# Nine octets of loads ahead, seven output buffers and whole-octet masked copies in a linear ReLU attention kernel

## The chip, the cores and the metric

The kernel runs on one core of a Trainium2 chip. Such a core has a matrix engine (TensorE, PE in the profile; its weight loads are PEld), a vector engine (VectorE, DVE), an activation engine (ScalarE, ACT), GpSimd (POOL), a synchronising engine (SyncE, SP) that here issues transfers and waits, and 16 DMA engines that move data between device memory (HBM) and the on-chip memory SBUF. PSUM is the small memory that TensorE writes its results to. The metric is the time of one execution on the device in microseconds (us), as the median of several runs; one more execution is recorded by the hardware profiler.

## The reference

```python
batch, heads, seq, dim = 8, 12, 512, 64        # float32
Q_feat = np.maximum(0, Q)
K_feat = np.maximum(0, K)
KV = np.einsum('bhkd,bhkv->bhdv', K_feat, V)
K_sum = np.sum(K_feat, axis=2)
numerator = np.einsum('bhqd,bhdv->bhqv', Q_feat, KV)
denominator = np.einsum('bhqd,bhd->bhq', Q_feat, K_sum)
return (numerator / (denominator[:, :, :, None] + 1e-10)).astype(np.float32)
```

There are 96 heads of 512 rows of 64 numbers. Each input and the output take 12.58 MB in HBM, so 50.3 MB have to be moved whatever the kernel does.

## The kernel before

**Tiling.** Eight heads make an "octet"; there are 12 octets (`NO`). One octet of an input is one contiguous piece of 1 MB in HBM, loaded by one DMA into a tile of 128 partitions x 2048 elements. The DMAs of GpSimd's queue turn float32 into bfloat16 on the way, so that a load writes 512 KB. In such a tile 16 partitions hold one head, and each partition holds 32 rows (`RQ`) of 64 numbers. Octet 0's K and V alone come over SP's queue as float32, into the output buffers 0 and 1 that nothing else uses yet. An output octet is float32, 1 MB, and is stored by one DMA (the last one by two halves).

**The work on one octet**, step by step:

- `copy_q` (line 198, VectorE) copies Q into the tile `q2`; TensorE transposes it in 16 steps (line 372) and ScalarE's `relu_q` (line 201) writes the result as `qt`.
- `prep_k` (line 183, VectorE) makes masked copies of relu(K) in `kf`; `prep_v` (line 194 on VectorE, line 192 on ScalarE) makes masked copies of V in `vo`. The masks keep the heads that share a partition group apart. There are two masks each (`s`, `t`), and before the change two halves of an octet (`g`), with a tile for each half: four K copies and four V copies of 128 x 1024 elements per octet. One of the V copies runs on ScalarE, seven copies run on VectorE.
- TensorE multiplies them to KV in 64 products (line 381), 32 for each half; ScalarE's `evac_kv` (line 209) brings KV to SBUF.
- TensorE forms the denominators and the eight heads' numerators (both through the helper on line 366, which writes to `ps_kv` and `ps_x`); ScalarE's `copy_ot` (line 217) copies the numerators to `ot`. TensorE transposes them back (line 390) in the next round of its loop.
- `denominators` (lines 222 to 229, VectorE) makes the reciprocals, and `norm` (line 234, VectorE) multiplies them into the output buffer, half an octet at a time. `store` (lines 244 and 247) sends the buffer off.

**What sets the order.** The programs of VectorE, ScalarE, GpSimd and SP are straight lists, written out by `body`, `setup` and `step(i)`; the class `Order` adds semaphore waits from what each operation reads and writes. TensorE runs a loop over the octets (`products`) and waits on counters that the others raise: `q2`, `dn`, `a0`, `d0`, `d1` ahead of the transposes of Q and the two halves of KV, `t0`, `t1` ahead of the transposes back, `n0`, `n1` ahead of the numerators. In `step(i)` octet i is multiplied, octet i-1 is normalised and stored, and octet i+1 is prepared: `first()` (Q copy and four of VectorE's copies) stands ahead of the norm of octet i-1, `second()` (three more) behind the denominators of octet i. In the step of i = 10 (`late`) both parts and ScalarE's V copy stand at the end.

**Queues and buffers.** GpSimd's queue first holds the Q of octet 0, then K, V and Q of octets 1 to 8 (`AHEAD` = 8), then by turns a store and the loads of one octet (store 0, octet 9, store 1, octet 10, store 2, octet 11). Ten semaphores (`LANES`) take turns on that queue, so that a DMA is issued only when the tenth before it has landed. The other stores are issued by SP, and each waits for the V of the last octet to have landed (line 246), then for its own data; SP's DMAs have four semaphores of their own (`sp`), and the last five stores one each (`last`). Octet o is written to output buffer (o + 2) mod `NOUT`, with `NOUT` = 8. At the end of `body` GpSimd waits for all the semaphores `pool` and `sp`; behind the closing handshake of the engines SP waits for the five `last` ones (line 419).

Of the kernel before, what the change touches and what calls it, by code (L numbers as in the profile page):

```python
# [89 lines left out]
def kernel(  # L90
# [16 lines left out]
    U = RQ // 2  # L107
    NO = NH // 8
    assert NO * 8 == NH and R == 16 and RQ == 32
    AHEAD = 8  # L110
    NI = AHEAD
    NOUT = 8
    LANES = 10

    fp32 = mybir.dt.float32
# [13 lines left out]
    ident32 = sb.tile([P, P], fp32, name="ident32")  # L129
    mask = sb.tile([P, 2, 2], fp32, name="mask")  # L130
    mask_h = sb.tile([P, 8, 2], fp32, name="mask_h")
    kf = [sb.tile([P, R, 2, D], bf16, name=f"kf{g}") for g in range(2)]
    vo = [sb.tile([P, R, 2, D4], bf16, name=f"vo{g}") for g in range(2)]
    kvf = sb.tile([P, 8 * 2 * D1], bf16, name="kvd")
    kvd = kvf.rearrange("p (h d) -> p h d", h=8)
    q2 = sb.tile([P, U, P], bf16, name="q2")
# [3 lines left out]
    den = sb.tile([P, RQ], fp32, name="den")  # L140
    rec = sb.tile([P, RQ], fp32, name="rec")
    q_sb = [sb.tile([P, U, P], bf16, name=f"q_sb{i}") for i in range(NI)]
    k_sb = [sb.tile([P, 2, R * D], bf16, name=f"k_sb{i}") for i in range(NI)]
    v_sb = [sb.tile([P, 2, R * D], bf16, name=f"v_sb{i}") for i in range(NI)]
    o_sb = [sb.tile([P, RQ, D], fp32, name=f"o_sb{i}") for i in range(NOUT)]
    ps_kv = psum.tile([P, 2, 512], fp32, name="ps_kv")
    ps_den = ps_kv[:, 1, 256:512]
# [12 lines left out]

    do = Order(nc, sems)

    def kv_src(g):
        o, j = g // 2, g % 2
        kv = (o_sb[0], o_sb[1]) if o == 0 else [x[o % NI].rearrange("p j (r d) -> p (j r) d", d=D) for x in (k_sb, v_sb)]
        key = [("o", c, j) if o == 0 else (c, o % NI, j) for c in ((0, 1) if o == 0 else "kv")]
        return kv[0][:, R * j:R * j + R], key[0], kv[1][:, R * j:R * j + R], key[1]

    def load_q(o):
        do.op("pool", lambda e: e.dma_start(out=q_sb[o % NI].rearrange("p u f -> p (u f)"), in_=Qr[o],  # L170
# [3 lines left out]
    def load(o):  # L174
        i = o % NI
        for n, X, t in (("K", Kr, k_sb), ("V", Vr, v_sb)):
            do.op("pool", lambda e: e.dma_start(out=t[i].rearrange("p j f -> p (j f)"), in_=X[o], single_packet=True),  # L177
                  writes=[(n.lower(), i, 0), (n.lower(), i, 1)], dma=lane("pool"))
        load_q(o)

    def prep_k(g, s):
        src, key, _, _ = kv_src(g)
        do.op("dve", lambda e: e.tensor_scalar(kf[g % 2][:, :, s, :], src, scalar1=0.0,  # L183
                                               scalar2=mask[:, 0, s:s + 1], op0=Alu.max, op1=Alu.mult),
              reads=[key, "mask"], writes=[("kf", g % 2, s)])

    def prep_v(g, t, who, sem=None):
        _, _, src, key = kv_src(g)
        to = vo[g % 2][:, :, t, 2:D + 2]
        m = mask[:, 1, t:t + 1]  # L190
        if who == "act":
            make = lambda e: e.activation(to, src, Act.Copy, scale=m)  # L192
        else:
            make = lambda e: e.tensor_scalar(to, src, scalar1=m, scalar2=None, op0=Alu.mult)  # L194
        do.op(who, make, reads=[key, "mask"], writes=[("vo", g % 2, t)], sem=sem)

    def copy_q(o):
        do.op("dve", lambda e: e.tensor_copy(q2, q_sb[o % NI]), reads=[("q", o % NI)], writes=["q2"], sem="q2")  # L198
# [32 lines left out]
    def norm(o, j):  # L231
        i = (o + 2) % NOUT
        rs = slice(16 * j, 16 * j + 16)
        do.op("dve", lambda e: e.tensor_tensor(o_sb[i][:, rs], ps_x[j].rearrange("p (r d) -> p r d", d=D),  # L234
                                               rec[:, rs].unsqueeze(2).to_broadcast([P, 16, D]), op=Alu.mult),
              reads=[("x", j), "rec"], writes=[("o", i, j)], sem=f"n{j}")

    def store(o, j=None):
        i = (o + 2) % NOUT
        rs = slice(0, RQ) if j is None else slice(16 * j, 16 * j + 16)  # L240
        to, src = Or[o].rearrange("p (r d) -> p r d", d=D)[:, rs], o_sb[i][:, rs]
        keys = [("o", i, h) for h in range(2) if j in (None, h)]
        if o + AHEAD + 1 < NO:
            do.op("pool", lambda e: e.dma_start(out=to, in_=src, single_packet=True), reads=keys, dma=lane("pool"))
        else:
            keys.append(("v", (NO - 1) % NI, 0))
            do.op("sp", lambda e: e.dma_start(out=to, in_=src), reads=keys, dma=lane("sp" if o < NO - 4 else "last"))

    KF = [[("kf", g, 0), ("kf", g, 1), ("vo", g, 0), ("vo", g, 1), ("vo1", g)] for g in range(2)]
    PK = [("pk", 0), ("pk", 1)]  # L250
    QT = [("qt", 0), ("qt", 1)]
    OT = [("ot", 0), ("ot", 1)]
# [4 lines left out]
    def body():  # L257
        for c, X in enumerate((Kr, Vr)):
            do.op("sp", lambda e: e.dma_start(out=o_sb[c].rearrange("p r d -> p (r d)"), in_=X[0]),
                  writes=[("o", c, 0), ("o", c, 1)], dma=lane("sp"))  # L260
        load_q(0)
        memset("pool", ident, 0.0, "ident")
        do.op("pool", lambda e: e.affine_select(out=ident, in_=ident, compare_op=Alu.not_equal, fill=1.0, base=0,
                                                pattern=[[-1, P]], channel_multiplier=1),
              reads=["ident"], writes=["ident"])
        for o in range(1, AHEAD + 1):
            load(o)
            if o == 1:
                setup()
        for o in range(NO + 1):  # L270
            step(o)
        nc.gpsimd.drain()
        for n in lanes["pool"] + lanes["sp"]:
            nc.gpsimd.wait_ge(sems[n], do.count[n])

    def setup():
        for h in range(4):
            for t in range(2):
                do.op("dve", lambda e: e.memset(mask[32 * h:32 * h + 32, 1, t:t + 1], 1.0 if h % 2 == t else 0.0),
                      writes=[("m", h, t), "mask"])  # L280
        for g in range(2):
            ones = vo[g][:, :, :, 1:D4 - 1]
            memset("dve", ones[:, :, :, 0:D + 2:D1], 0.0, ("vo1", g))
            for h in range(4):
                memset("dve", ones[32 * h:32 * h + 32, :, h % 2, 0:D + 2:D1], 1.0, ("vo1", g))
        do.op("dve", lambda e: e.tensor_copy(ident32, ident), reads=["ident"], writes=["ident32"],
              sem="dn")
        for c in range(2):
            do.op("dve", lambda e: e.tensor_reduce(
                out=mask_h[:, :, c], in_=ident32.rearrange("p (h b) -> p h b", h=8), op=Alu.add,  # L290
                axis=mybir.AxisListType.X), reads=["ident32"], writes=[("mh", c), "mask_h"])
        do.op("dve", lambda e: e.tensor_reduce(
            out=mask[:, 0, :], in_=mask_h[:, :, 0].rearrange("p (a s) -> p s a", s=2), op=Alu.add,
            axis=mybir.AxisListType.X), reads=["mask_h"], writes=["mask"])
        prep_k(0, 0)
        prep_k(0, 1)
        prep_v(0, 0, "dve", "d0")
        prep_v(0, 1, "act", "a0")
        do.op("dve", lambda e: e.memset(kvf.bitcast(fp32)[:, 0:4 * D1], 0.0), writes=KVD, sem="n0")
        do.op("dve", lambda e: e.memset(kvf.bitcast(fp32)[:, 4 * D1:], 0.0), writes=KVD, sem="n1")  # L300
        copy_q(0)
        prep_k(1, 0)
        prep_k(1, 1)
        prep_v(1, 0, "dve")
        prep_v(1, 1, "dve", "d1")
        for j in range(2):
            nc.scalar.sem_inc(sems[f"t{j}"], 1)
            do.note("act", "act", (), (), f"t{j}", 1)

    def step(i):  # L310
        r = i + 1
        more, last, late = i + 1 < NO, i == NO, i == NO - 2

        def first():
            copy_q(i + 1)
            prep_k(2 * i + 2, 0)
            prep_k(2 * i + 2, 1)
            prep_v(2 * i + 2, 0, "dve", "d0")
            prep_k(2 * i + 3, 0)

        def second():
            prep_k(2 * i + 3, 1)
            prep_v(2 * i + 3, 0, "dve")
            prep_v(2 * i + 3, 1, "dve", "d1")

        if not last:
            do.looped([("q2", r)], ["q2", "ident"], [("pq", 0)])
# [3 lines left out]
            do.looped([("dn", r), ("a0", r), ("d0", r)], KF[0], PK + ["pd"])  # L331
            do.looped([("d1", r)], KF[1], PK + ["pd"])
            evac_kv()
            if more and not late:
                prep_v(2 * i + 2, 1, "act", "a0")
                first()
        if i > 0:
            o = i - 1
            do.looped([("t0", r), ("t1", r)], [*OT, "ident32"], [("x", 0)])
# [9 lines left out]
        if not last:  # L349
            do.looped([("qt", r), ("ev", r)], [*QT, *KVD], ["pd"])  # L350
            denominators()
            for j in range(2):
                do.looped([(f"n{j}", r)], [*QT, *KVD], [("x", j)])
            copy_ot(0, "act")
            copy_ot(1, "act" if more else "dve")
            if late:
                prep_v(2 * i + 2, 1, "act", "a0")
                first()
            if more:
                second()  # L360

    def products():
        pe = nc.tensor
# [4 lines left out]
        with pe.Fori(0, NO + 2, 1) as r, pe.If(r > 0):  # L368
            with pe.If(r < NO + 1):
# [5 lines left out]
                for g in range(2):  # L375
                    for s in ("dn", "a0", "d0") if g == 0 else ("d1",):
                        pe.wait_ge(sems[s], r)
                    for k in range(R):
                        for h in range(2):
                            ps = slice(64 * h, 64 * h + 64)  # L380
                            x = pe.matmul(  # L381
                                ps_kv[:, h, 0:2 * (D + 2)].rearrange("p (t d) -> p t d", t=2),
                                kf[g][ps, k, :, :].rearrange("p s d -> p (s d)"), vo[g][ps, k, :, 1:D4 - 1],
                                start=(g + k == 0), stop=(g == 1 and k == R - 1), skip_group_check=True)
                    x.then_inc(sems["pe"], 1)
            with pe.If(r > 1):
# [62 lines left out]
```

## Time and profile before

| | |
|---|---|
| runs | 126.50, 126.62 and 127.31 us (median 126.62) |
| the profiled execution | 126.42 us, of which the span from the first to the last instruction is 124.6 us |
| mean granted TensorE clock | 0.934 |
| busy, share of the span | PE 70%, PEld 60%, VectorE 70%, ScalarE 63%, GpSimd 17% |
| DMA queues | software (GpSimd's): 20.97 MB written; hardware (SP's): 11.54 MB written |
| norm of half an octet (line 234, VectorE) | 24 times, 1.214 us |
| masked K copy, bfloat16, 128 x 1024 (line 183, VectorE) | 44 times, 0.458 us |
| masked V copy, bfloat16, 128 x 1024 (line 194, VectorE; line 192, ScalarE) | 33 times, 0.481 us; 11 times, 1.153 us |
| Q copy, bfloat16, 128 x 2048 (line 198, VectorE) | 12 times, 0.683 us |
| a load of GpSimd's queue, from issue to landing | median 24.3 us |
| a store of SP's queue, from issue to landing | median 8.6 us for 1 MB, 3.2 us for half |

The profile shows one execution: for each engine the instructions with their start and length, for each idle time what ended it, and for the 16 DMA engines the share of time in which they moved something. Times within it are counted from the span's start. Durations of instructions on one engine can overlap the next one by some 0.1 us, so that the distance between two starts is often less than the duration.

### The profile page before, as it was taken

How to read it: one execution, taken by the hardware profiler on the slowest of the kernel's cores; microseconds unless marked ns; L12 is line 12 of the kernel's file. 1: busy time of each engine (PE TensorE's matmuls, PEld its weight loads, DVE VectorE, ACT ScalarE, POOL GpSimd, SP SyncE). 2: the span in 40 equal slices, each digit the busy share in tenths (PEclk: the TensorE clock that was granted, in tenths of full speed). 3: DMA queues.
4: the chain of work that ended last, by engine and by line, in shares of the span. 5: the costliest groups of instructions: out<-in, count | busy, mean ns of one | idle time of the engine just before them, and what ended most of it. 6: DMA issues, size and time to landing. Idle time of an engine off the chain costs nothing.

```text
span 124.6 us, 3458 instructions
## 1 busy us (share of the span) xinstructions
PE 87.3 (70%) x1440; PEld 74.8 (60%) x1440; DVE 87.2 (70%) x181; ACT 78.3 (63%) x108; POOL 21.1 (17%) x43
## 2 busy tenths in 40 slices
PE   0000394997997979989797998928966994892900
PEld 0000393996795959779596885915963982781900
DVE  2440947749799898989989799099189359658330
ACT  0000765968988889898888988835773848743000
POOL 5931211321131122113211321000000000000000
PEclk9999999679999999999999999995996799999595
DMA  2999999999999999999999999999999999999971
GB/s 53 400 316 233 212 213 213 213 212 216 216 212 213 213 214 210 213 217 214 212 213 216 368 218 218 334 256 216 301 292 214 268 417 423 426 426 434 426 296 75
DMA packets 7061, 32.56 MB, mean 261 GB/s; under 512 B 784, under 2 KB 784, under 8 KB 5392
## 3 DMA queue, kind: packets, MB, share of 16 engines
q0 software_dynamic: 5328, 20.97, 77.4%
q1 hardware_dynamic: 1728, 11.54, 22.4%
q14 instruction: 4, 0.03, 0.1%
q8 instruction: 1, 0.02, 0.0%
HBM read 37.75 MB, written 12.58 MB: 404 GB/s over the span
## 4 chain that ended last, share of the span: by engine, by line
DMA 58%; DVE 16%; PE 14%; POOL 4%; issue 4%; DVEq 0%; POOLq 0%; SPq 0%
DMA q_sb<-in_Q_dram 20%; DMA v_sb<-in_V_dram 20%; DMA k_sb<-in_K_dram 19%; DVE o_sb L234 8%; PE ps_x L390 5%; PE ps_kv L381 4%; DVE kf L183 3%; PE ps_qt L372 3%; PE ps_x L366 2%; DVE vo L194 2%; POOL q_sb L170 1%; POOL v_sb L177 1%; DVE ot_sb L217 1%; POOL k_sb L177 1%; DVE den L226 1%
## 5 line engine op out<-in xcount | busy, mean ns | idle before, releaser
L234 DVE TENSOR_TENSOR o_sb<-ps_x,rec 128x1024 f32<-128x1024 f32 x24 | 28.3, 1214 | 8.4 <-PE ps_x L390 8.4
L217 ACT COPY ot_sb<-ps_x 128x1024 f32<-128x1024 f32 x23 | 23.2, 1012 | 12.3 <-PE ps_x L366 11.2
L381 PE MATMUL ps_kv<-vo,kf 64*128 64x132 bf16 x768 | 27.1, 229 | 0.6 <-DVE vo L194 0.6
L372 PE MATMUL ps_qt<-ident,q 128*128 128x128 bf16 x192 | 15.9, 248 | 16.5 <-DVE q L198 15.6
L390 PE MATMUL ps_x<-ident,ot_sb 128*128 128x128 f32 x192 | 25.2, 288 | 1.7 <-DVE ot_sb L217 1.7
L381 PEld LDWEIGHTS ps_kv<-vo,kf 64*128 64x128 bf16 x768 | 24.8, 100 | 2.3 <-issue 0.9
L372 PEld LDWEIGHTS ps_qt<-ident,q 128*128 128x128 bf16 x192 | 13.9, 113 | 19.1 <-DVE q L198 15.9
L390 PEld LDWEIGHTS ps_x<-ident,ot_sb 128*128 128x128 f32 x192 | 22.3, 148 | 3.2 <-issue 2.0
L209 ACT CAST kvd<-ps_kv 64x260 bf16<-64x260 f32 x48 | 17.9, 374 | 9.3 <-PE ps_kv L381 8.4
L201 ACT ACTIVATE qt<-ps_qt 128x1024 bf16<-128x1024 bf16 x24 | 23.3, 1030 | 0.6 <-PE ps_qt L372 0.6
L366 PE MATMUL ps_x<-qt,kvd 128*128 128x256 bf16 x96 | 16.0, 296 | 10.9 <-DVE o_sb L234 9.9
L183 DVE TENSOR_SCALAR kf<-k_sb,mask 128x1024 bf16<-128x1024 bf16 x44 | 19.1, 458 | 0.0
L198 DVE COPY q<-q_sb 128x2048 bf16<-128x2048 bf16 x12 | 8.2, 683 | 13.9 <-DMA q_sb<-in_Q_dram 13.9
L366 PEld LDWEIGHTS ps_x<-qt,kvd 128*128 128x128 bf16 x96 | 7.9, 102 | 16.3 <-DVE o_sb L234 15.4
L194 DVE TENSOR_SCALAR vo<-v_sb,mask 128x1024 bf16<-128x1024 bf16 x33 | 14.9, 481 | 0.0
L192 ACT ACTIVATE vo<-v_sb,mask 128x1024 bf16<-128x1024 bf16 x11 | 12.7, 1153 | 0.3
L170 POOL DMA_DIRECT2D q_sb<-in_Q_dram x12 | 6.7, 558 | 16.1 <-DMA v_sb<-in_V_dram 9.5
L177 POOL DMA_DIRECT2D k_sb<-in_K_dram x11 | 6.3, 575 | 17.7 <-DMA q_sb<-in_Q_dram 13.8
L192 ACT ACT_TABLE_LOAD x1 | 1.3, 1283 | 12.5 <-DMA o_sb<-in_V_dram 12.5
L177 POOL DMA_DIRECT2D v_sb<-in_V_dram x11 | 6.1, 555 | 15.6 <-DMA k_sb<-in_K_dram 9.9
L366 PE MATMUL ps_kv<-kvd,qt 128*128 128x16 bf16 x192 | 6.9, 179 | 1.8 <-ACT kvd L209 1.8
L366 PEld LDWEIGHTS ps_kv<-kvd,qt 128*128 128x128 bf16 x192 | 6.0, 96 | 2.6 <-issue 1.9
(21 smaller groups left out, 27.0 us busy)
## 6 DMA issues: line engine op xcount, KB each, us to landing
out_dram<-o_sb SPq DMA_DIRECT2D x8, 1024.0 KB, 8.6
q_sb<-in_Q_dram POOLq DMA_DIRECT2D x12, 512.0 KB, 24.3
k_sb<-in_K_dram POOLq DMA_DIRECT2D x11, 512.0 KB, 24.3
v_sb<-in_V_dram POOLq DMA_DIRECT2D x11, 512.0 KB, 24.3
out_dram<-o_sb POOLq DMA_DIRECT2D x3, 1024.0 KB, 24.5
o_sb<-in_K_dram SPq DMA_DIRECT2D x1, 1024.0 KB, 6.6
o_sb<-in_V_dram SPq DMA_DIRECT2D x1, 1024.0 KB, 11.1
out_dram<-o_sb SPq DMA_DIRECT2D x2, 512.0 KB, 3.2
```

Of the source, the lines that this page charges most:

```text
L177: do.op("pool", lambda e: e.dma_start(out=t[i].rearrange("p j f -> p (j f)"), in_=X[o], single_packet=True), writes=[(n.lower(), i, 0), (n ...
L183: do.op("dve", lambda e: e.tensor_scalar(kf[g % 2][:, :, s, :], src, scalar1=0.0, scalar2=mask[:, 0, s:s + 1], op0=Alu.max, op1=Alu.mult), ...
L192: make = lambda e: e.activation(to, src, Act.Copy, scale=m)
L194: make = lambda e: e.tensor_scalar(to, src, scalar1=m, scalar2=None, op0=Alu.mult)
L201: do.op("act", lambda e: e.activation(qt[:, j * (U // 2):(j + 1) * (U // 2)], ps_qt[j], Act.Relu), reads=[("pq", j)], writes=[("qt", j)], ...
L209: do.op("act", lambda e: e.copy(kvd[64 * c:64 * c + 64, s:8:2, c * D1:c * D1 + D1].rearrange("p (g t) d -> p g t d", t=2), ps_kv[64 * s:64 ...
L217: do.op(who, lambda e: e.copy(to, src) if who == "act" else e.tensor_copy(to, src), reads=[("x", j)], writes=[("ot", j)], sem=f"t{j}")
L234: do.op("dve", lambda e: e.tensor_tensor(o_sb[i][:, rs], ps_x[j].rearrange("p (r d) -> p r d", d=D), rec[:, rs].unsqueeze(2).to_broadcast( ...
L366: return pe.matmul(out_, lhsT, rhs, start=True, stop=True, skip_group_check=True)
L372: x = pe.transpose(ps_qt[u // 8][:, u % 8, :], q2[:, u, :], ident)
L381: x = pe.matmul(ps_kv[:, h, 0:2 * (D + 2)].rearrange("p (t d) -> p t d", t=2), kf[g][ps, k, :, :].rearrange("p s d -> p (s d)"), vo[g][ps, ...
L390: x = pe.transpose(ps_x[u // 8][:, u % 8 * P:u % 8 * P + P], ot[:, u].rearrange("p h c -> p (h c)"), ident32)
```

## The change

Loads run nine octets ahead (`AHEAD` 9, and as many input buffers); there are seven output buffers (`NOUT` 7). `kf` and `vo` become one tile each for the whole octet. VectorE's K copies and one of its V copies take the whole octet (128 x 2048); of the other V mask ScalarE still copies the first half and VectorE the second: two K copies and two V copies per octet on VectorE. In `step` the Q copy and both K copies stand ahead of the norm, and VectorE's V copies behind the denominators; the different order for i = 10 is gone. With `AHEAD` 9, two stores stay on GpSimd's queue (`o + AHEAD + 1 < NO`). SP waits for the semaphores `pool` and `sp`, instead of GpSimd.

```diff
-    AHEAD = 8
+    AHEAD = 9
     NI = AHEAD
-    NOUT = 8
+    NOUT = 7
...
-    kf = [sb.tile([P, R, 2, D], bf16, name=f"kf{g}") for g in range(2)]
-    vo = [sb.tile([P, R, 2, D4], bf16, name=f"vo{g}") for g in range(2)]
+    kf = sb.tile([P, RQ, 2, D], bf16, name="kf")
+    vo = sb.tile([P, RQ, 2, D4], bf16, name="vo")
...
+    def prep_k(o, s):
+        src, key = kv_src(o)[0]
+        do.op("dve", lambda e: e.tensor_scalar(kf[:, :, s, :], src, scalar1=0.0, scalar2=mask[:, 0, s:s + 1],
+                                               op0=Alu.max, op1=Alu.mult),
+              reads=[key, "mask"], writes=[("kf", s)])
+
+    def prep_v(o, t, halves, who, sem=None):
+        src, key = kv_src(o)[1]
+        rs = slice(R * halves[0], R * halves[-1] + R)
+        to, src, m = vo[:, rs, t, 2:D + 2], src[:, rs], mask[:, 1, t:t + 1]
...
-            nc.gpsimd.wait_ge(sems[n], do.count[n])
+            nc.sync.wait_ge(sems[n], do.count[n])
...
         prep_k(0, 0)
         prep_k(0, 1)
-        prep_v(0, 0, "dve", "d0")
-        prep_v(0, 1, "act", "a0")
+        prep_v(0, 1, (0,), "act", "a0")
+        prep_v(0, 0, (0, 1), "dve", "d0")
+        prep_v(0, 1, (1,), "dve", "d1")
...
         copy_q(0)
-        prep_k(1, 0)
-        prep_k(1, 1)
-        prep_v(1, 0, "dve")
-        prep_v(1, 1, "dve", "d1")
...
-        more, last, late = i + 1 < NO, i == NO, i == NO - 2
-
-        def first():
-            copy_q(i + 1)
-            prep_k(2 * i + 2, 0)
-            prep_k(2 * i + 2, 1)
-            prep_v(2 * i + 2, 0, "dve", "d0")
-            prep_k(2 * i + 3, 0)
-
-        def second():
-            prep_k(2 * i + 3, 1)
-            prep_v(2 * i + 3, 0, "dve")
-            prep_v(2 * i + 3, 1, "dve", "d1")
+        more, last = i + 1 < NO, i == NO
...
             evac_kv()
-            if more and not late:
-                prep_v(2 * i + 2, 1, "act", "a0")
-                first()
+            if more:
+                prep_v(i + 1, 1, (0,), "act", "a0")
+                copy_q(i + 1)
+                prep_k(i + 1, 0)
+                prep_k(i + 1, 1)
...
             copy_ot(1, "act" if more else "dve")
-            if late:
-                prep_v(2 * i + 2, 1, "act", "a0")
-                first()
             if more:
-                second()
+                prep_v(i + 1, 0, (0, 1), "dve", "d0")
+                prep_v(i + 1, 1, (1,), "dve", "d1")
...
-                                kf[g][ps, k, :, :].rearrange("p s d -> p (s d)"), vo[g][ps, k, :, 1:D4 - 1],
+                                kf[ps, R * g + k, :, :].rearrange("p s d -> p (s d)"), vo[ps, R * g + k, :, 1:D4 - 1],
```

## The prediction, made before the change was run

> **What bounds the kernel now.** I read the share of each engine first (no engine is busy over 70% of the span), then the DMA rows of the 40 slices and the HBM line. In the slices, DMA is the busy share of the 16 DMA engines in tenths; in the next line GB/s count the written bytes, so that a load, which turns float32 into bfloat16, shows 213 where a store shows 426.
>
> ```profile
> DMA  2999999999999999999999999999999999999971
> GB/s 53 400 316 233 212 213 213 213 212 216 216 212 213 213 214 210 213 217 214 212 213 216 368 218 218 334 256 216 301 292 214 268 417 423 426 426 434 426 296 75
> HBM read 37.75 MB, written 12.58 MB: 404 GB/s over the span
> DMA 58%; DVE 16%; PE 14%; POOL 4%; issue 4%; DVEq 0%; POOLq 0%; SPq 0%
> ```
>
> The DMA engines never rest from the second slice to the 38th: this kernel is a stream of 50.3 MB. The last line, the chain of waits, is DMA for its first 80 us and compute for the last 44. So I need to know which of the two really sets the end. The next view gives stretches at the end: length, busy time of PE, PEld, DVE, ACT, POOL, then granted clock, DMA share and GB/s.
>
> ```profile
> 103.00:106.00 3.00, 1.38 (x17) 0.97 (x17) 2.93 (x8) 2.74 (x3) 0.00 (x0) 1.00 1.00 421
> 112.00:115.00 3.00, 0.86 (x7) 0.31 (x4) 2.89 (x5) 1.01 (x1) 0.00 (x0) 1.00 1.04 437
> 118.00:119.00 1.00, 0.65 (x4) 0.35 (x2) 0.70 (x2) 0.00 (x0) 0.00 (x0) 0.80 0.57 238
> 119.00:121.00 2.00, 0.00 (x0) 0.00 (x0) 0.91 (x1) 0.00 (x0) 0.00 (x0) 1.00 0.81 332
> 121.00:122.00 1.00, 0.00 (x0) 0.00 (x0) 0.00 (x0) 0.00 (x0) 0.00 (x0) 0.91 1.01 414
> ```
>
> DMA stays full until 118 and has only small holes then. GpSimd's timeline shows the order of its queue and its pace; an entry is start, length, what, and the idle time before it with its releaser (the landing of the transfer ten before).
>
> ```profile
> 68.63 0.54 POOL L244 DMA_DIRECT2D out_dram<-o_sb  x1 [1.93 <-DMA v_sb<-in_V_dram]
> 71.16 0.62 POOL L177 DMA_DIRECT2D k_sb<-in_K_dram  x1 [2.00 <-DMA q_sb<-in_Q_dram]
> 73.59 0.53 POOL L177 DMA_DIRECT2D v_sb<-in_V_dram  x1 [1.81 <-DMA out_dram<-o_sb]
> 76.01 0.53 POOL L170 DMA_DIRECT2D q_sb<-in_Q_dram  x1 [1.89 <-DMA k_sb<-in_K_dram]
> ```
>
> Each transfer, load or store, takes one place of 2.46 us (73.59 to 76.01, and the same all along). Octet 11's Q, issued at 76.01, lands 24.5 us later, at 100.5; V of octet 11 lands just before 97.98, where SP, which waits for it, issues its first store. These are VectorE's rows at the end:
>
> ```profile
> 90.76 0.69 DVE L198 COPY q<-q_sb 128x2048 bf16<-128x2048 bf16 x1 [3.02 <-DMA q_sb<-in_Q_dram]
> 101.21 2.35 DVE L234 TENSOR_TENSOR o_sb<-ps_x,rec 128x1024 f32<-128x1024 f32 x2 [3.64 <-PE ps_x L390]
> 110.36 2.35 DVE L234 TENSOR_TENSOR o_sb<-ps_x,rec 128x1024 f32<-128x1024 f32 x2 [2.31 <-PE ps_x L390]
> 118.69 1.23 DVE L234 TENSOR_TENSOR o_sb<-ps_x,rec 128x1024 f32<-128x1024 f32 x1 [0.30 <-PE ps_x L390]
> ```
>
> The DMA rows tell from issue to landing: SP's first store (octet 3, issued 97.98) 5.0 us, octet 10's (112.74) 7.7, octet 11's two halves (118.41 and 119.94) 3.3 and 3.0. So octet 10 lands at 120.4, the halves at 121.7 and 122.97. From 102.96 to 120.44 seven stores land, 2.497 us each, and each half lands 1.25 to 1.3 after what was before it, which is that same pace. Both limits meet: the last store is ready just as DMA becomes free. 1.6 us of closing follow to 124.6, and 1.8 lie outside the span (profiled execution 126.42; the median of three is 126.62, 0.2 above it).
>
> **The change part by part.** *Queue order.* GpSimd's queue now holds octets 1 to 9, then store 0, octet 10, store 1, octet 11: 36 transfers instead of 37. Nothing before octet 9 moves. K, V, Q of octets 9, 10 and 11 land 2.46 us earlier: Q at 78.4, 88.2 and 98.0, V of octet 11 at 95.5. Store 2 goes to SP, where ten stores stand in place of nine. The bytes are the same: minus one place of 2.46, plus one of 2.497, +0.04 on the last landing if compute delivers in time.
>
> *Seven output buffers.* Octet o uses buffer (o+2) mod 7. Octets 7, 8, 9 now wait for stores 0, 1, 2; octets 10 and 11 for 3 and 4. By the queue, stores 0 and 1 land one place after Q of octets 9 and 10, at 80.8 and 90.6. VectorE is ready for those norms 2.0 us after each Q (below), so it waits 0.4 to 0.5 us twice; Q of the next octet comes 9.8 us after the last, where the octet takes about 7.6, and that hides it. Store 2 is SP's first: 95.5 + 5.0 = 100.5.
>
> *Whole-octet copies.* Half copies stand 0.40 us apart on VectorE (its rows 42.06, 42.85, 43.25, 43.65); the only whole-octet bfloat16 copy, of Q, takes 0.61 to the next start (41.45 to 42.06). A whole masked copy lies between 0.61 and 0.79; I take 0.66, as 1024 more elements cannot add more than the Q copy's whole rate allows (0.61/2048 per element, 0.31) and two fixed parts become one. Per octet two K copies are 1.32 instead of 1.58, V 0.66 + 0.40 instead of 1.2: 0.4 less on VectorE, of 7.3. But two waits get tighter. K copies now need the whole KV product to be done, not its first half, and the product needs the whole V copy, which is now after the denominators. In steady state before (norm at 43.65) the denominators end at 47.08, the product runs 47.76 to 49.83, the norm follows at 50.98, 2.2 after Q landed. Now: V copy 47.08 + 0.66 = 47.75, product as before to 49.85, K copies to 51.2: one octet per 7.55 us (7.8 with 0.79), where loads come every 7.39. This lags 0.2 to 0.4 an octet, up to 3 us over octets 2 to 8, and the two gaps of 2.46 behind octets 9 and 10 give 4.9 back before the end.
>
> *The last octet.* Its K copies now stand before octet 9's norm. Q lands 98.0, copy 0.61, K 1.32: 100.0; store 2 makes it 100.5 (101.21 before). The next norm comes 7.35 later (denominators 3.4, V 0.7, product 2.05, transposes 1.04, hand-overs 0.15), at 107.9, instead of 9.15, at 110.36: there the old order had put eight copies of octet 11 between. From there to the last norm's end it was 9.56, and that code is the same: 117.4 instead of 119.92. A window of half granted clock on the way (PEclk 0.50 stood at 95 to 98 and 115 to 118 after PE had idled) stretches this by 1.3 to 1.6: 119.0.
>
> *Waits on SP.* After its last issue SP now waits for 14 lanes, all landed by then; behind them stand the closing handshake (0.4 us, 120.31 to 120.72) and the five last waits. SP's event instructions stand 0.07 apart, so at most 1.0 us; with the issue (0.35) it is 1.8, inside the 3.0 from issue to landing. GpSimd's waits had no price: after its last issue at 76.01 nothing is queued behind them. At the start five of ten memsets go, and two more float32 halves of V (0.72 each) come ahead of octet 0's Q copy, which moves from 13.82 to about 15.2; VectorE's waits for Q at 19.22 (2.1) and 26.66 (2.1) take that up; without them it would be 1.4 on every octet, still under the lag of 4.9 that is given back.
>
> *Sum.* Compute is ready 0.9 to 2.5 us earlier, and DMA doesn't get shorter: the gain is capped by the holes at the end, (188 + 2 x 94 + 12) / 426 = 0.91 us. The halves' landings at full pace say that the slowest DMA engine had no hole: 0. I take the latter nearly whole, -0.15. With +0.04: 126.42 - 0.1 = 126.3.
>
> **Rivals.** *Store 2 is late (slower).* Octet 9's norm waits for the first SP store, and everything behind it on VectorE stands still. It decides once that norm starts after 103.0 (119.92 - 9.56 - 7.35). If store 2 shares the engines with those issued behind it and lands like the median SP store, 9.4 us after issue, the norm starts at 104.9 and the end is 1.9 later, 128.3. For it: this wait did not exist. Against: stores land one after another, 2.5 apart, and the first took 5.0 beside the same last load. V and Q of octet 11 landed 2.5 apart although a store was issued between. The Trainium skill (DMA: Bandwidth & Descriptors, Queues, rings and completion order) says that each DMA engine takes turns between the queues it has work for, packet by packet; by that, Q of octet 11 could be held back by stores. The trace doesn't agree by its landings. Were Q held until store 2 lands, at 100.5, the norm would start at 102.5: still inside 103.0, but by 0.5 only. Chance 0.17, spread from 126.4 to 128.3.
>
> *The chain of waits is right (faster).* It runs through the loads on GpSimd's queue; one place less there moves every later step, so 126.42 - 2.46 = 124.0. For it: the chain, 58% DMA. Against: DMA share 1.0 to 118; the removed store must still be moved. Chance 0.08.
>
> *Octets take longer than thought.* With K copies waiting for the product, a period of 8.24 us (from the norm at 28.86, nine octets to 103.0) would make compute the bound: 0.45 more than my worst. Chance 0.04, about 128.
>
> **How the numbers follow.** Forecast, DMA-bound and unchanged: 0.71, 125.5 to 126.8 (all holes closed; the median's 0.2 above the profile and as much again). The two slower cases, 0.21, are half below 127.9; the faster 0.08. A measurement of this kernel can tell about 1% from no change: 125.35 and 127.89. Faster 0.09, within 0.79, slower 0.12. The range 125.3 to 127.9 leaves out 0.08 below and 0.11 above.
>
> **What would show it.** In the changed profile: Q of octet 11 copied at 98, octet 9's norm at 100.5 released by a store; the next norm near 108; last norm's end at 117 to 119; DMA share near 1.0 to 121 and the last landing at 122.1 to 123. I am wrong if the last landing moves by over 1 us while DMA share falls before 118, or if octet 9's norm starts after 103.

## The result, and the profile after

The changed kernel takes 125.81 us (median of 14 runs, 125.58 to 126.17), the kernel before, in the same sessions, 126.69 us (14 runs, 126.14 to 127.50). The ratio is 0.992 with a 95% interval of 0.990 to 0.994: 1.0 us faster (0.7 to 1.3). The forecast was 126.3 us, "within 1%", range 125.3 to 127.9. The profiled execution took 125.64 us with a span of 123.7, against 126.42 and 124.6: 0.9 us less in the span.

The page's DMA rows after the change, to be laid beside those of before: a share of 0.9 or more up to the 39th slice, with 416 GB/s where 296 stood.

```profile
DMA  3999999999999999999999999999999999999991
GB/s 72 401 310 225 213 216 212 212 212 216 216 213 215 213 213 213 212 213 213 212 216 212 212 212 272 331 215 238 352 212 212 378 424 427 424 424 424 424 416 77
HBM read 37.75 MB, written 12.58 MB: 407 GB/s over the span
```

The same stretches at the end (length, the engines' busy time, granted clock, DMA share, GB/s) show that the holes of before at 118 to 121 (shares 0.57 and 0.81) are closed, and that most DMA engines are done about 1 us sooner:

```profile
118.00:119.00 1.00, 0.00 (x0) 0.00 (x0) 0.88 (x1) 0.00 (x0) 0.00 (x0) 1.00 0.92 381
119.00:121.00 2.00, 0.00 (x0) 0.00 (x0) 0.00 (x0) 0.00 (x0) 0.00 (x0) 0.93 1.00 410
121.00:122.00 1.00, 0.00 (x0) 0.00 (x0) 0.00 (x0) 0.00 (x0) 0.00 (x0) 0.50 0.21 82
```

VectorE's timeline has the steps that the prediction named: the Q copy of octet 11 at 98.07, both K copies ahead of octet 9's norm, that norm at 100.51 released by a store, the next one at 109.37 (near 108 was forecast), the end of the last one at 118.89. (The first row names TensorE as the releaser; octet 11's Q had landed at 97.98, just ahead of it.)

```profile
98.07 0.69 DVE L197 COPY q<-q_sb 128x2048 bf16<-128x2048 bf16 x1 [2.90 <-PE ps_x L373]
98.68 1.41 DVE L182 TENSOR_SCALAR kf<-k_sb,mask 128x2048 bf16<-128x2048 bf16 x2
100.51 2.35 DVE L233 TENSOR_TENSOR o_sb<-ps_x,rec 128x1024 f32<-128x1024 f32 x2 [0.42 <-DMA out_dram<-o_sb]
109.37 2.36 DVE L233 TENSOR_TENSOR o_sb<-ps_x,rec 128x1024 f32<-128x1024 f32 x2 [4.37 <-PE ps_x L373]
117.66 1.23 DVE L233 TENSOR_TENSOR o_sb<-ps_x,rec 128x1024 f32<-128x1024 f32 x1 [0.25 <-PE ps_x L373]
```

In the trace's completion records the last store lands at 122.58 instead of 122.97: 0.39 us. From there to the end of the span it takes 1.12 us instead of 1.63: another 0.51. The prediction had this second part, the closing, as the same before and after. It is visible among SP's waits of the last microseconds (engine, line, waited for: total, times, longest). Before:

```profile
SPq L419 <- DMA out_dram<-o_sb: 2.2, 2, 1.2
SPq L444 <- PEq L444: 1.3, 2, 1.1
```

After:

```profile
SPq L402 <- DMA out_dram<-o_sb: 2.3, 2, 1.2
SPq L427 <- PEq L427: 0.8, 2, 0.6
```

SP's last waits for stores are alike; the second handshake of the engines, after them (line 444, now 427), holds SP for 0.8 us instead of 1.3. (The view puts it down to TensorE; GpSimd's own closing instructions show where it goes: from its first event behind the handshake to its clearing of the semaphores it takes 0.74 us before, 0.22 after.)

### The profile page after: what moved, and what is told of

It reads as the page before. It is cut to its first block, busy times and chain, and to the rows that moved or that the text cites. A ratio compares the mean times of both kernels' runs of the same rounds, so it can differ in the third digit from the quotient of the medians.

```text
span 123.7 us, 3422 instructions
## 1 busy us (share of the span) xinstructions
PE 85.6 (69%) x1440; PEld 73.4 (59%) x1440; DVE 83.2 (67%) x140; ACT 78.6 (64%) x108; POOL 22.8 (18%) x42
## 4 chain that ended last, share of the span: by engine, by line
DMA 77%; PE 8%; DVE 7%; POOL 2%; issue 2%; POOLq 0%; DVEq 0%; SPq 0%
DMA v_sb<-in_V_dram 39%; DMA q_sb<-in_Q_dram 20%; DMA k_sb<-in_K_dram 14%; DVE o_sb L233 5%; DMA out_dram<-o_sb 4%; PE ps_x L373 4%; PE ps_kv L364 2%; PE ps_qt L355 2%; POOL q_sb L169 1%; DVE ot_sb L216 1%; PE ps_x L349 0%; POOL v_sb L176 0%; POOL k_sb L176 0%; DVE den L225 0%; DVE rec L228 0%
## 5 line engine op out<-in xcount | busy, mean ns | idle before, releaser
L355 PE MATMUL ps_qt<-ident,q 128*128 128x128 bf16 x192 | 15.1, 242 | 16.4 <-DVE q L197 15.4
L364 PE MATMUL ps_kv<-vo,kf 64*128 64x132 bf16 x768 | 26.1, 225 | 0.5
L364 PEld LDWEIGHTS ps_kv<-vo,kf 64*128 64x128 bf16 x768 | 24.2, 97 | 2.3 <-issue 2.2
L355 PEld LDWEIGHTS ps_qt<-ident,q 128*128 128x128 bf16 x192 | 13.1, 110 | 19.2 <-DVE q L197 15.4
L349 PE MATMUL ps_x<-qt,kvd 128*128 128x256 bf16 x96 | 15.3, 287 | 11.6 <-DVE o_sb L233 11.5
L182 DVE TENSOR_SCALAR kf<-k_sb,mask 128x2048 bf16<-128x2048 bf16 x22 | 15.6, 750 | 7.2 <-PE ps_kv L364 7.2
L193 DVE TENSOR_SCALAR vo<-v_sb,mask 128x2048 bf16<-128x2048 bf16 (+1 forms) x22 | 11.6, 571 | 0.0
L169 POOL DMA_DIRECT2D q_sb<-in_Q_dram x12 | 7.6, 634 | 15.9 <-DMA v_sb<-in_V_dram 11.1
L176 POOL DMA_DIRECT2D k_sb<-in_K_dram x11 | 7.2, 651 | 17.5 <-DMA q_sb<-in_Q_dram 14.0
```

Of the source, the lines that this page charges most:

```text
L176: do.op("pool", lambda e: e.dma_start(out=t[i], in_=X[o], single_packet=True), writes=[(n.lower(), i)], dma=lane("pool"))
L182: do.op("dve", lambda e: e.tensor_scalar(kf[:, :, s, :], src, scalar1=0.0, scalar2=mask[:, 0, s:s + 1], op0=Alu.max, op1=Alu.mult), reads= ...
L349: return pe.matmul(out_, lhsT, rhs, start=True, stop=True, skip_group_check=True)
L355: x = pe.transpose(ps_qt[u // 8][:, u % 8, :], q2[:, u, :], ident)
L364: x = pe.matmul(ps_kv[:, h, 0:2 * (D + 2)].rearrange("p (t d) -> p t d", t=2), kf[ps, R * g + k, :, :].rearrange("p s d -> p (s d)"), vo[p ...
```

## The experiments

The theory after the result (A in the expectations): two independent terms. The closing is 0.5 us shorter, because GpSimd no longer waits for the semaphores. And compute ends earlier against the stream, so that the last stores follow without holes: up to 0.4 us. The rivals: the closing differs by chance; compute still sets the end; the whole-octet copies carry the gain, or the last octet's order does. Ratios are to the kernel before, measured in the same session.

**1. SP's waits alone, on the kernel before (`b_sp_waits`).**

```diff
-            nc.gpsimd.wait_ge(sems[n], do.count[n])
+            nc.sync.wait_ge(sems[n], do.count[n])
```

> The kernel before with one part of the change alone: SP instead of GpSimd waits for the semaphores of both queues. Two readings of the 0.5 us by which the changed kernel's closing (last landing to end of span) is shorter, 1.1 instead of 1.6. Theory A, GpSimd's waits cost at the very end, by what GpSimd still has to do after a long list of waits: closing 1.1, last landing as before (122.9 to 123.0), 0.5 us faster, ratio 0.996. Rival B, the closing differs by chance from one execution to the next: closing 1.6, ratio 1.000.

Measured: 126.33 us, ratio 0.998 (0.995 to 1.0005). The profile has a span of 124.1, the last landing at 122.97 as before, a closing of 1.12:

```profile
SPq L419 <- DMA out_dram<-o_sb: 2.2, 2, 1.2
SPq L444 <- PEq L444: 0.8, 2, 0.6
```

The closing is as theory A says; the ratio's interval just includes 1, so that this run alone shows no gain in the time.

**2. GpSimd's waits put back in the changed kernel (`a_pool_waits`).** The same edit the other way.

> The changed kernel with GpSimd waiting for the semaphores again, all else as changed. Theory A (these waits lengthen the closing): closing 1.6 behind a last landing at 122.6, 0.5 us slower than the changed kernel, ratio to the kernel before 0.996. Rival B (chance): closing 1.1, ratio 0.992 as the changed kernel.

Measured: 126.14 us, ratio 0.994 (0.991 to 0.996), closing 1.64. That is 0.33 us above the changed kernel's median (measured in another session; the ratios, 0.994 and 0.992, are 0.2 us apart with intervals that overlap). The handshake again:

```profile
SPq L402 <- DMA out_dram<-o_sb: 2.9, 2, 1.7
SPq L427 <- PEq L427: 1.3, 2, 1.1
```

Chance is out: in all profiles of this study the closing is 1.63 or 1.64 where GpSimd waits at the end (four kernels, the one before among them) and 1.12 where SP does (nine), but for experiment 9.

**3. Nine ahead and seven buffers alone, on the kernel before (`b_ahead9`).**

```diff
-    AHEAD = 8
+    AHEAD = 9
...
-    NOUT = 8
+    NOUT = 7
```

> The kernel before with nine octets ahead and seven output buffers alone; half copies, the old order for the last octet and GpSimd's waits stay. Theory A (the queue order brings the last loads 2.46 us earlier, compute ends earlier and the holes at the DMA's end close): norm of octet 9 at 100.5 released by store 2, the next one 9.15 later at 109.7, last norm's end at 119.2 (119.92 before), last landing 122.6, closing 1.6; 0.3 us faster, ratio 0.997. Rival C (it is the whole-octet copies that end the compute earlier, and the queue order is worth nothing): last norm's end at 119.9, last landing 123.0, ratio 1.000.

Measured: 126.43 us, ratio 0.997 (0.995 to 0.999), closing 1.64. So the order of the queue, with the seven buffers that it needs, is worth something by itself, 0.4 us (0.1 to 0.6), and rival C falls in its strict form. In the profiled execution (126.70 us, one of the two slowest of twelve) the norm of octet 9 starts at 101.13 released by a store, and the last one ends at 120.64 rather than at 119.2: the stream there had lost 0.6 us on its way (one load, at 78.96, landed 3.0 us after the one before, not 2.46).

**4. The other parts without the queue order (`a_ahead8`).** The changed kernel with `AHEAD = 8` and `NOUT = 8`.

> The changed kernel with eight octets ahead and eight output buffers: whole-octet copies, the order with the last octet's K copies ahead of octet 9's norm, and SP's waits stay. Theory A: Q of octet 11 lands at 100.5, the norm of octet 9 starts at 102.5, the next at 111.4 (8.86 later as in the changed kernel, 7.35 at full granted clock: 109.9), last norm's end 119.4 to 120.9, last landing 122.8 to 124.0, closing 1.1: between 0.6 us faster and 0.6 slower than before, ratio 0.995 to 1.005. Rival C (the whole copies are what gains): last landing 122.6, ratio 0.992.

Measured: 126.53 us, ratio 0.998 (0.9955 to 1.001), closing 1.12. With the closing's gain in it, it still is no faster than experiment 1: the whole-octet copies with the new order gain nothing without the earlier loads. The profiled execution (127.62 us, the slowest of its twelve) shows why they can lose: octet 9's norm waits behind the copies of octet 11 until 103.48, the last one ends at 121.86, and the stream stands nearly still for want of stores:

```profile
119.00:121.00 2.00, 1.60 (x9) 1.34 (x7) 1.59 (x2) 0.00 (x0) 0.00 (x0) 0.67 0.23 94
121.00:122.00 1.00, 0.00 (x0) 0.00 (x0) 0.86 (x1) 0.00 (x0) 0.00 (x0) 1.00 0.79 328
```

Share 0.23 where the changed kernel has 1.00: a compute end as late as this, 22.9 us behind a common mark of the stream where the changed kernel has 20.9 (table below), does cost time. It is no test of the prediction's threshold (octet 9's norm after 103.0), because the stream of this execution itself was 1 us late.

**5. Compute earlier (`a_warm`).** In the last round, ahead of TensorE's wait for the copies:

```diff
+            with pe.If(r > NO):
+                for u in range(U + 6):
+                    pe.transpose(ps_qt[u % U // 8][:, u % 8, :], q2[:, u % U, :], ident)
```

> The changed kernel with 22 more transposes of an old Q tile on TensorE in its last round, into a PSUM tile that nobody reads any more, while it waits for the copy ahead of the last transposes back, so that the clock gate stays open there (those took 3.5 us at half granted clock). Theory A (the stream of transfers sets the end, compute has slack): last norm's end 1.0 to 1.5 us earlier, 117.4 to 117.9, last landing 122.6 as in the changed kernel, same time (within 0.2 us). Rival D (compute still sets the end): 1.0 to 1.5 us faster, ratio to the kernel before 0.981 to 0.984.

Measured: 125.80 us, ratio 0.993 (0.990 to 0.996). The last transposes back take 1.94 us instead of 3.49, the last norm ends at 117.71 instead of 118.89, and the time is the changed kernel's, 125.81. Compute 1.2 us earlier gains nothing.

```profile
114.19 1.94 PE L376 MATMUL ps_x<-ident,ot_sb 128*128 128x128 f32 x16
115.36 2.36 DVE L233 TENSOR_TENSOR o_sb<-ps_x,rec 128x1024 f32<-128x1024 f32 x2 [1.32 <-PE ps_x L376]
```

**6. Compute later (`a_slow`).**

```diff
+    own32 = sb.tile([P, 1024], fp32, name="own32")
...
+            if not more:
+                for _ in range(1):
+                    do.op("dve", lambda e: e.tensor_copy(own32, ps_x[1]), reads=[("x", 1)], writes=["own32"])
             copy_ot(1, "act" if more else "dve")
```

> The changed kernel with one more copy of 128x1024 from PSUM on VectorE (1.16 us) ahead of the last octet's second copy: everything behind it, up to the last norm, comes 1.2 us later (last norm's end 120.1, halves issued at 118.6 and 120.1). Theory A (the stream sets the end until the last store is issued later than 3.0 us ahead of the stream's own end): the last half lands 3.0 to 3.2 after its issue, at 123.1 to 123.3, 0.5 to 0.7 us slower than the changed kernel. Rival D (compute sets the end): 1.2 us slower, last landing 123.8.

Measured: 125.78 us, ratio 0.992 (0.989 to 0.995): not even the expected 0.5 us. The added copy is in the path:

```profile
113.58 1.16 DVE L343 COPY own<-ps_x 128x1024 f32<-128x1024 f32 x1
114.66 1.21 DVE L217 COPY ot_sb<-ps_x 128x1024 f32<-128x1024 f32 x1
118.06 1.23 DVE L234 TENSOR_TENSOR o_sb<-ps_x,rec 128x1024 f32<-128x1024 f32 x1 [2.19 <-PE ps_x L377]
```

The expectation missed in that 3.0 us is not the shortest way from issue to landing. It is 2.6 us where the queue has nearly run out (2.58 for the last half of this run), so that a half may be issued 0.4 us later without harm. Experiments 5 and 6 together show that the changed kernel's end is set by the stream, with over 1 us of slack for compute.

**7. The old order for the last octet (`a_late`).**

```diff
-            if more:
+            if more and i != NO - 2:
...
+            if i == NO - 2:
+                prep_v(i + 1, 1, (0,), "act", "a0")
+                copy_q(i + 1)
+                prep_k(i + 1, 0)
+                prep_k(i + 1, 1)
```

> The changed kernel with the old order for the last octet: its Q and K copies stand behind octet 9's norm and the denominators instead of ahead of the norm. Theory A (octet 9's norm waits for store 2, at 100.5, whatever stands ahead of it, and compute has slack): norm at 100.5, the next about 0.3 to 1.0 later than in the changed kernel's 109.4, last landing 122.6 to 122.9, same time within 0.3 us. Rival E (the order of the last octet is part of the gain): the next norm later by the 1.9 us of copies, last norm's end at 120.8, last landing 123.8, 1.2 us slower.

Measured: 126.20 us, ratio 0.992 (0.989 to 0.996). Octet 9's norm starts at 100.25, again released by a store; the next at 110.41, 10.2 later, not 8.9; the last ends 1.0 us later than in the changed kernel. The ratio shows no loss; the median is 0.4 above that of experiments 5 and 6 of the same session. A loss of some tenths stays possible; rival E's 1.2 us is out.

**8. Six output buffers (`a_nout6`).** `NOUT = 6`.

> The changed kernel with six output buffers: octet 8's norm, not octet 9's, waits for SP's first store. This is the slower rival of the prediction made real, one octet earlier. Theory A: norm of octet 8 at 100.5 released by a store, octets 9 and 10 at periods of 7.6 to 8.9, 108 to 109 and 116 to 118, last norm's end at 125.5 to 127.5, last landing 3.0 later, 128.5 to 130.5: 6 to 8 us slower than the changed kernel. If the buffers' waits were covered, it would be the changed kernel's time.

Measured: 130.67 us, ratio 1.03 (1.02 to 1.04): 4.9 us above the changed kernel. Octet 8's norm is released by SP's first store, 10 us after where it stood:

```profile
100.54 2.35 DVE L233 TENSOR_TENSOR o_sb<-ps_x,rec 128x1024 f32<-128x1024 f32 x2 [2.07 <-DMA out_dram<-o_sb]
```

The mechanism of the slower rival is real and begins one buffer further on. The size is below the expected 6 to 8: the next two octets took 8.3 and 7.4 us, the last norm ended at 124.8, and the last store landed 2.6 after its issue.

**9. GpSimd's list longer, but not its waiting (`a_pool_len`).** The changed kernel with

```diff
+        for n in 2 * lanes["pool"][:7]:
+            nc.gpsimd.wait_ge(sems[n], 16)
         for o in range(NO + 1):
             step(o)
```

> The changed kernel with 14 more waits on GpSimd in the middle of its list, all of them for loads that have landed long before, so that they hold up nothing. Two readings of the closing's 0.5 us. Theory G (what matters is how long GpSimd's list is: a piece of its program is fetched just then): closing 1.5 to 1.7, and an instruction transfer near the end. Theory H (what matters is that GpSimd waits for stores late): closing 1.1.

Measured: 126.20 us, ratio 0.996 (0.9935 to 0.999), closing 1.50, 0.4 us above the changed kernel. The handshake, where no wait for a late store is left on GpSimd:

```profile
SPq L404 <- DMA out_dram<-o_sb: 2.3, 2, 1.2
SPq L429 <- PEq L429: 1.2, 2, 1.0
```

So what costs is not that GpSimd waits late, nor for what, but that its list is longer. The trace's records say where. In the kernel before and in experiments 2, 3, 9 and 10 GpSimd pauses for 0.40 to 0.44 us in its closing, ahead of three different instructions, and it is the 69th of GpSimd's records each time, in lists of 70 to 73. With SP's waits the lists have 63 or 65 records and end before that place. So the pause belongs to a place in GpSimd's list. That a piece of its program is fetched there would fit; the instruction transfers of the trace mostly fall after the span's end and do not show it, so what happens in the pause remains open.

**10, 11. Compute earlier on the kernel before, without and with SP's waits (`b_warm`, `b_warm_sp`).** The edits of 5, and of 5 and 1.

> The kernel before, with nothing of the change, and 22 more transposes of an old Q tile on TensorE in its last round, into a PSUM tile that nobody reads any more; in the changed kernel these shortened the last transposes back and brought the last norm 1.2 us forward. Theory A (a compute end about 1 us earlier closes the holes in the last stores, however it is brought about; the closing is another matter): last norm's end 118.6 (119.92 before), last landing 0.3 to 0.5 earlier at 122.5 to 122.7 where the stream is as in the kernel before, closing 1.6; ratio 0.996 to 0.997. Rival F (the holes close only because a store was moved from GpSimd's queue to SP's): last landing as before, ratio 1.000. Rival D (compute sets the end): ratio 0.990.

> As the run before, and SP instead of GpSimd waits for the semaphores of both queues: two small edits, without the new queue order, the seven buffers or the whole-octet copies. Theory A (two independent terms, the closing's 0.5 and the holes' 0.4): closing 1.1, holes closed, ratio 0.992 to 0.994, as fast as the changed kernel. Rival F (the queue order and the copies carry the gain): closing 1.1 alone, ratio 0.996 to 0.998.

Measured: 126.59 us, ratio 1.000 (0.9975 to 1.002), and 126.19 us, ratio 0.997 (0.995 to 0.999). As a test of the holes these failed: compute was not brought forward. The last transposes back took 1.94 us as meant, but the window of half granted clock fell on octet 11's products (2.91 us, 2.24 before), octet 10's norm came at 111.56 instead of 110.36, and the last norm ended at 119.84. Share 0.57 and 0.56 stands at 118 to 120 in the first profile: the holes stayed and so did the time. Nothing follows for or against the queue order from that. The pair does show the closing's term once more: 0.40 us between the medians of one session, 1.63 against 1.12 in the profiles.

**12. A try for a faster version (`a_act_v0`).**

```diff
-            do.op("sp", lambda e: e.dma_start(out=o_sb[c].rearrange("p r d -> p (r d)"), in_=X[0]),
+            do.op(("sp", "act")[c], lambda e: e.dma_start(out=o_sb[c].rearrange("p r d -> p (r d)"), in_=X[0]),
```

> The changed kernel with octet 0's V loaded by ScalarE's queue, issued at the same time as K by SP instead of 0.44 us behind it. A try for a faster version, since only the stream and its start are left: DMA share is under one half until 2.75 us. If the first transfers' own start is what the stream waits for, everything moves forward by up to 0.3 us, ratio 0.990; if the DMA engines are full with K alone, the time of the changed kernel, ratio 0.992.

Measured: 125.97 us, ratio 0.994 (0.992 to 0.9965): no gain over the changed kernel. No version of this study beats it.

**The stream's own time.** The profiles differ by up to 1.3 us in how far the stream has come before the end, so last landings are best compared from a common mark. From the landing of the 36th transfer of GpSimd's queue (97.97 before, 97.98 after; 97.70 to 98.95 over all profiles), 10 MB are left in every version: ten stores in the new order, octet 11's Q and nine stores in the old one. Time from there to the last landing:

| kernel | us | last norm's end, from the same mark |
|---|---|---|
| changed kernel; `a_warm`; `a_pool_waits`; `a_pool_len` | 24.61; 24.61; 24.61; 24.61 | 20.9; 19.4; 20.8; 20.9 |
| `a_act_v0` | 24.75 | 19.3 |
| `b_ahead9` | 24.65 | 22.0 |
| `b_sp_waits`; `b_warm_sp` | 24.74; 24.80 | 21.1; 21.5 |
| `a_slow`; `a_late` | 24.78; 24.84 | 22.2; 22.2 |
| before; `b_warm` | 25.01; 25.10 | 21.9; 21.8 |
| `a_ahead8` | 25.52 | 22.9 |
| `a_nout6` | 29.44 | 26.8 |

Ten stores at the pace of the changed kernel's (2.455 us) are 24.55. Four versions stand within 0.1 us of that floor; `a_act_v0`, whose compute ended earliest, stands 0.2 us above it, so that the stream alone scatters by that much. In the new order, compute that ends up to 22.2 us behind the mark costs at most 0.25 us. With 22.9 (`a_ahead8`, the old order) the stream takes 0.9 us longer than in the changed kernel.

Experiment 3 has holes (share 0.61 at 119 to 121) and takes 24.65 all the same. The records of the landings show how. A transfer has 16 completion marks, as many as there are DMA engines, and in the full stream the last three come late: for octet 10's store in the kernel before, thirteen at 118.82 to 119.01, three at 119.91, 120.12 and 120.44. The holes there are the waiting of engines that are ahead. At the end of the kernel before, the last mark still comes 0.48 us behind the thirteenth (122.97 and 122.49). In experiments 3, 4, 6, 7 and 8 this is 0.05 us or less: the lead was used up, and by this reading only then does a later store move the end. (A mark does not name its engine; that the same ones stay behind is inferred.)

So of the 0.4 us that the profiled execution of the kernel before stands above the changed kernel, the holes explain little: there octet 10's store and octet 11's two halves land within 5.03 us, 0.12 above the pace. The greater part is the stream's own stumbling earlier on (one landing 2.59 and one 2.53 us after the one before), and theory A's second term is not shown as it was put.

## Why the prediction was right, and what it missed

The forecast was no change, 0.1 us less than the profiled execution, and the one after the change took 0.8 less. The bound and the lack of harm were foreseen. That the time fell within the range is owed to the range's width, since the sum left out most of the gain.

*What bounds the kernel.* Right: the stream sets the end. Experiments 5 and 6 move compute by 1.2 us either way, and the time stays.

*Queue order.* Right: Q of octet 11 was copied at 98.07 (98.0 forecast), and the removed place came back as a tenth store. With the seven buffers it is worth 0.4 us alone (experiment 3), not the 2.46 of the second rival.

*Seven buffers.* Right for octet 9, whose norm came at 100.51 with a wait of 0.42 us. The two waits of 0.4 to 0.5 us for stores 0 and 1 did not come about: these landed at 80.63 and 90.65, as forecast, but VectorE, lagging, came to octet 7's norm 2.2 us later and started octet 8's 0.02 us after store 1 had landed, with no idle time that its row shows.

```profile
82.82 2.35 DVE L233 TENSOR_TENSOR o_sb<-ps_x,rec 128x1024 f32<-128x1024 f32 x2
90.67 2.36 DVE L233 TENSOR_TENSOR o_sb<-ps_x,rec 128x1024 f32<-128x1024 f32 x2
```

The slower rival (store 2 late) fell, as store 2 landed 4.9 us after its issue; with six buffers it costs 4.9 us of time.

*Whole-octet copies.* The K copy took 0.665 us (two from 81.49 to 82.82), 0.66 forecast. The period was mis-sized: 7.80 us an octet instead of 7.55. VectorE's timeline, with the wait that the prediction named, for the whole product:

```profile
73.68 1.42 DVE L182 TENSOR_SCALAR kf<-k_sb,mask 128x2048 bf16<-128x2048 bf16 x2 [1.24 <-PE ps_kv L364]
75.01 2.48 DVE L233 TENSOR_TENSOR o_sb<-ps_x,rec 128x1024 f32<-128x1024 f32 x2
```

The norm before it started at 67.21, the product at 71.57 (TensorE's row), 4.36 later rather than 4.13 (47.78 less 43.65 by the forecast), and the K copies waited 1.24 us for its end. As forecast, the two gaps of the stream hid this lag.

*The last octet.* The first value, 107.9 for octet 10's norm, was too early; the case beside it, a window of half granted clock, came true. TensorE stood idle for 2.47 us before octet 10's numerators, waiting for the norm that waited for the store, and the granted clock was 0.61 at 103 to 106: 109.37, and the last norm's end at 118.89 (117.4 to 119.0 forecast). The rows after, TensorE's and the stretch's:

```profile
101.79 0.61 PE L349 MATMUL ps_x<-qt,kvd 128*128 128x256 bf16 x4 [2.47 <-DVE o_sb L233]
103.00:106.00 3.00, 2.90 (x32) 2.42 (x34) 1.94 (x5) 2.78 (x4) 0.00 (x0) 0.61 1.02 429
```

*Waits on SP.* The half about SP was right: its 14 waits took 0.44 us, hidden. (Octet 0's Q copy at the start moved to 14.69, not 15.2, and was hidden as well.) The half about GpSimd is the step that failed: "GpSimd's waits had no price: after its last issue at 76.01 nothing is queued behind them." On GpSimd's list they cost 0.5 us in the closing, by their number (experiment 9), and that is half of the gain in the span. The page couldn't price it, but the prediction carried the 1.6 us of closing over as fixed without asking which engine's instructions it consists of.

*Sum.* The closing was given 0, and was 0.5. The holes were given 0.15 of at most 0.91 us; the last landing came 0.39 earlier, and by the table above little of that is holes: the reading that the slowest DMA engine had none fits the late marks, and 0.15 was about the most that holes could give (0.12 by the landings above). Together that is the 0.9 us of the span. Open: what makes the other half of the gain in the medians. The queue order alone is 0.4 us faster in the time (experiment 3, 0.1 to 0.6), though its profile doesn't show by what. More slack for compute in executions that stumble would fit the scatter of the runs (126.14 to 127.50 before, 125.58 to 126.17 after), but experiment 6 took the slack away and ten of its twelve runs stayed within 125.67 to 125.84, so that this is only argued. Whether the whole-octet copies add anything is open too (experiments 2 and 3: 0.994 and 0.997, with intervals that overlap).

## What to carry to other kernels

Where a stream of transfers is full nearly to the end, a faster compute is worth next to nothing; ask how late the last store may be issued, and stop there. Reading ahead by taking a buffer from the output is safe only while the store that frees it lands about when the next result is ready: here, with seven buffers, octet 9 waited 0.4 us for SP's first store, hidden; with six, octet 8 waited for that same store, and it cost 4.9 us of time. Holes in the mean share of the DMA engines cost nothing while the engines that wait are ahead of the last ones. And the microseconds after the last landing belong to the kernel too: here moving 14 waits from GpSimd's list to SP's took 0.5 us off them.

## What the hardware showed that was not expected

The closing depends on the length of GpSimd's list by 0.4 to 0.5 us (1.12 against 1.50 to 1.64), whatever the added instructions wait for: the pause of 0.40 to 0.44 us stands ahead of the 69th record in all five profiled kernels whose list reaches that far.

Half a store (512 KB) needs 2.6 us from issue to landing when the queue has nearly run out (2.58 to 2.65 in experiments 4, 6 and 8), less than the 3.0 that looked like the shortest in the profile before.

Queues share the DMA engines in some places and not in others. Octet 0's K and V, both from SP, land one behind the other in the changed kernel:

```profile
o_sb<-in_K_dram SPq DMA_DIRECT2D x1, 1024.0 KB, 6.2
o_sb<-in_V_dram SPq DMA_DIRECT2D x1, 1024.0 KB, 10.7
```

With V on ScalarE's queue (experiment 12) they land together, K 4.3 us later than it had:

```profile
o_sb<-in_V_dram ACTq DMA_DIRECT2D x1, 1024.0 KB, 10.2
o_sb<-in_K_dram SPq DMA_DIRECT2D x1, 1024.0 KB, 10.5
```

The Trainium skill (DMA: Bandwidth & Descriptors, Queues, rings and completion order) says that a DMA engine takes turns between the queues it has work for, by packets; experiment 12 agrees. At the end, though, Q of octet 11 on GpSimd's queue (issued as a single packet) landed 2.46 us after V, at its usual pace, with three of SP's stores issued in between: there the stores did not take turns with it. What made the difference, the kind of queue, the single packet or its issue 24 us earlier, was not tested.
